# Where the input norm's squares, sums and rotary tables run: ScalarE and VectorE in place of POOL

## The chip, the cores and the metric

The kernel runs on one core of a Trainium2 chip. The core has a matrix engine (TensorE, PE in the profile), VectorE (DVE), ScalarE (ACT), GpSimd (POOL) and a queue engine that issues transfers (SyncE, SP). The metric is the device time of one launch in microseconds, and lower is better. The time quoted is the median of a few runs.

## The reference

An encoder block normalises its input, multiplies it with one wide matrix, and feeds three mixers (dilated window attention, grouped-query attention, attention into a memory), whose gated outputs are projected, merged and projected once more. What matters here is the beginning:

```python
def rms_norm(x, g):
    y = xf * lax.rsqrt(jnp.mean(xf * xf, axis=-1, keepdims=True) + NORM_EPS)
    return (y * g.astype(jnp.float32)).astype(x.dtype)

h = rms_norm(x, g_pre[layer])
a_qkv, bq, bk, bv, mq, ga, gb, gm, mg = jnp.split(h @ w_in[layer], split_at, axis=-1)
...
qb_ = axial_rope(rms_norm(bq.reshape(b, s, B_HEADS, HEAD_DIM), q_norm[layer]), row_pos, col_pos)
kb_ = axial_rope(rms_norm(bk.reshape(b, s, B_KV_HEADS, HEAD_DIM), k_norm[layer]), row_pos, col_pos)
```

`x` has 1024 rows of 1024 channels, in float32. The block needs the sum of squares of each row, and for the second mixer tables of cosine and sine multiplied with the norm weights of queries and keys.

## The kernel before

The input comes transposed, as eight tiles `xk[0]` to `xk[7]` of 128 channels by 1024 rows. Float32 products are made of two parts: each operand is split into a high part (`hh`, `wh`, made by ACT) and the rest (`hl`, `wl`, made by DVE as source minus high part), and three multiplications are added up (high times high, rest times high, high times rest).

**The x stage** is a loop over the eight tiles. For every other tile, `split_wkv` splits a quarter of the key and value weights (`wbh` on ACT, `wbl` on DVE, line 106). Then `x_tile(k)` makes `hh[k]` on ACT (L271) and `hl[k]` on DVE (L272), both scaled by the norm's weight, in two halves of 512 columns. Then `x_sq(k - 1)` squares the tile before, in place, and adds it to `acc`, so that `acc` ends as the sum over the eight channel groups. The first square is written to `acc` itself (L276). Squares of tiles 2 and 4 run on POOL (L279), the others on ACT (L281). The sums of tiles 1, 3, 5, 6 and 7 run on DVE, those of 2 and 4 on POOL (both L282). Behind the loop come the key tables `Ck` and `Sk` on POOL (L464) and the last square and sum, of tile 7. The row scale isn't applied to `x`; it is applied later to what comes out of the multiplications.

**PE meanwhile** runs `kv_proj`: for each tile k, 24 multiplications of 128x256 (eight row blocks times three terms, L373) into four banks. Ahead of those of k = 7 stands `rstd_cols`: eight transposes of `acc` (L258), two reductions on DVE (L259) into `rcol`, and then on POOL scale and offset (L128), the power -1/2 (L130), `rsq` (L380, L381) and `nrcol` (L382).

**Behind it** PE goes on with two gate units. Each is two halves of 24 multiplications of 128x512 into one of two banks `d`. A half is evacuated by DVE (L220, multiplied with `rb`, the row scale as a row), ACT (L221, tanh) and DVE (L222); the third half needs the bank of the first, the fourth that of the second. Woven in between are the norm of the keys, `k_norm` (a square on ACT, L335, a reduction on DVE, L337, four small operations on `kss` on POOL, L338 to L341, and the products with the key tables on DVE, L342 to L346), the transposes that make `rb` (L264, copied by ACT, L423) and the preparation of the memory `mt` (`mh`, `ml`, L393 and L394, its squares on ACT, L395, and sums on POOL, L396 to L399). `kn_mult` then multiplies keys with `kss` (L405) and splits the values (`VS`, L410 and L411). Then eight small units (L537) follow that work on the memory.

**What sets the order.** PE's order is that of the program throughout. For ACT, DVE and POOL the order is the program's from the x stage to the end of the two gate units (`manual_schedule`); what is written behind that, `kn_mult` and the query tables `Cq` and `Sq` (L464) among it, is placed by a scheduler that works with estimated times and may put an operation into a gap ahead of its place in the program. Each engine then works through its instructions in the order fixed beforehand. Loads and stores are issued by SP in order.

Of the kernel before, what the change touches and what calls it, by code (L numbers as in the profile page):

```python
# [10 lines left out]
AF = mybir.ActivationFunctionType  # L11
OP = mybir.AluOpType
# [11 lines left out]
B_COS, B_SIN, B_QN, B_QS, B_KN, B_KS = 0, 512, 170, 234, 298, 362  # L24
# [26 lines left out]
def block(ctx: ExitStack, tc: tile.TileContext, x, xT, memT, cst, msk, bcst, tabA, gpost,  # L51
          wu, wb, wmem, wbr, wout, out):
    nc = tc.nc
    V, A, G, PE = nc.vector, nc.scalar, nc.gpsimd, nc.tensor
# [24 lines left out]
    def pss1():  # L79
        return bank["p"].tile([P, 512], F32, name="s1", tag="s1", bufs=bank["n"][1])  # L80
# [4 lines left out]
    def pso():  # L85
        return bank["p"].tile([P, 512], F32, name="ov", tag="o", bufs=bank["n"][3])
# [11 lines left out]
    rcol = const.tile([P, NT], F32, name="rcol")  # L98
    nrcol = const.tile([P, NT], F32, name="nrcol")
# [27 lines left out]
    def rstd_of(dst, ssq, n, post=None):  # L127
        G.tensor_scalar(dst, ssq, 1.0 / n, EPS, op0=OP.mult, op1=OP.add)  # L128
        w = dst.shape[-1]
        G.tensor_tensor(dst, dst, mhalf[:, :w], op=OP.pow)  # L130
        if post is not None:
            G.tensor_scalar(dst, dst, post, None, op0=OP.mult)
# [70 lines left out]
    fp = {}  # L203
# [48 lines left out]
    xk = [st.tile([P, S], F32, name=f"xk{k}") for k in range(8)]  # L252
    acc = st.tile([P, S], F32, name="acc")

    def cols_of(col, acc, n):
        p = pst()
        for T in range(n):
            PE.transpose(p[:, T, :], acc[:, T * 128:T * 128 + 128], ident)  # L258
        V.tensor_reduce(col, p[:, :n], axis=AX.X, op=OP.add)  # L259
# [14 lines left out]
    def x_sq(k):  # L274
        if k == 0:
            A.activation(acc, xk[k], AF.Square)  # L276
        else:
            if k in P_SQ:
                G.tensor_tensor(xk[k], xk[k], xk[k], op=OP.mult)  # L279
            else:  # L280
                A.activation(xk[k], xk[k], AF.Square)  # L281
            (V if k in V_ADD else G).tensor_tensor(acc, acc, xk[k], op=OP.add)  # L282


    def fetch_wb(c0):
# [77 lines left out]
    def kv_proj():  # L363
        banks = [pss1(), pss1(), pss1(), pso()]
        th, tl = wkv
        for k in range(8):
            if k == 7:
                rstd_cols()
            for T in range(NT):
                dst = banks[T // 2][:, T % 2 * 256:T % 2 * 256 + 256]  # L370
                t = slice(T * 128, T * 128 + 128)
                for i, (a, b) in enumerate([(hh[k][:, t], th[:, k]), (hl[k][:, t], th[:, k]), (hh[k][:, t], tl[:, k])]):
                    PE.matmul(dst, a, b, start=k == 0 and T % 2 == 0 and i == 0, stop=k == 7 and T % 2 == 1 and i == 2)  # L373
        return banks

    def rstd_cols():
        for i in range(2):
            cols_of(rcol[:, 4 * i:4 * i + 4], acc[:, i * 512:i * 512 + 512], 4)
        rstd_of(rcol, rcol, D)
        G.tensor_tensor(rsq, rcol, rcol, op=OP.mult)  # L380
        G.tensor_scalar(rsq, rsq, 1.0 / HD, None, op0=OP.mult)  # L381
        G.tensor_scalar(nrcol, rcol, -1.0, None, op0=OP.mult)  # L382

    mh, mlo, mm, part, kns = [], [], [], [], []

# [15 lines left out]
    def kn_mult(n):  # L401
        t1, ss = part[n]
        kn = st.tile([P, 2, 2, 64], F32, name="kn", bufs=4)
        kns.append(kn)
        V.tensor_tensor(kn, t1, ss[:, :, :, None].to_broadcast([P, 2, 2, 64]), op=OP.mult)  # L405
        for t in range(2):
            T = 2 * n + t
            vv = banks[n].rearrange("q (t h d) -> q t h d", t=2, h=4)[:, t, 2:4]
            r = rcol[:, T:T + 1]
            A.activation(VS[:, T, :, 0:64], vv, AF.Copy, scale=r)  # L410
            V.scalar_tensor_tensor(VS[:, T, :, 64:128], vv, r, VS[:, T, :, 0:64].bitcast(F32),  # L411
                                   op0=OP.mult, op1=OP.subtract)
# [50 lines left out]
    def table(nm, src, gv, E):  # L463
        E.tensor_tensor(tabs[nm], bt[:, src:src + 512].rearrange("p (t d) -> p t d", t=NT),  # L464
                        cs[:, gv:gv + 64][:, None, :].to_broadcast([P, NT, 64]), op=OP.mult)

    for k in range(8):
        if k % 2 == 0:
            split_wkv(k // 2)
        x_tile(k)  # L470
        if k:
            x_sq(k - 1)
    table("Ck", B_COS, B_KN, G)
    table("Sk", B_SIN, B_KS, G)
    x_sq(7)
    banks = kv_proj()
    fp["p"] = st
    add_gate(2, 0)
# [10 lines left out]
        late.append(lambda n=n: kv_out(n, kns[n]))  # L489
    for n in range(4):  # L490
        kn_mult(n)
    table("Cq", B_COS, B_QN, G)
    table("Sq", B_SIN, B_QS, G)

    def mem_norm_a():
        mm.append(st.tile([P, 2], F32, name="col"))
# [780 lines left out]
MN_A, MN_B = 0, 7  # L1277
KV_K = 5
WR, KV_STEP, RB_WAIT, KN_PAD = 2, 700, 1500, 2800.0
V_ADD, P_SQ = (1, 3, 5, 6, 7), (2, 4)  # L1280
LAG_S, LAG_T, LAG_P, LAG_F = 9, 10, 12, 13
BP = 4
B_LEAD, B_PRIO = 1.0, 120
# [118 lines left out]
```

## Time and profile before

| What | us |
|---|---|
| median of 3 runs | 1536.92 |
| their lowest and highest | 1534.99, 1537.64 |
| the profiled execution | 1537.39 |
| its span, first to last instruction | 1535.6 |
| TensorE busy in the span | 1498.6 |
| VectorE, ScalarE, POOL busy | 972.8, 712.7, 443.9 |
| last sum of squares ends | 38.73 |
| gate units begin on PE | 44.92 |
| memory units begin on PE | 68.45 |

The times in the profile count from the first instruction. A timeline row gives the start, the busy time, the engine, the line, the operation with output and inputs, their shapes, how many, and in brackets the idle time before it with what ended it. Busy times of neighbours can overlap by some hundredths, so the step from start to start is a little shorter than the busy time. The granted clock is the share of TensorE's full speed.

### The profile page before, as it was taken

How to read it: one execution, taken by the hardware profiler on the slowest of the kernel's cores; microseconds unless marked ns; L12 is line 12 of the kernel's file. 1: busy time of each engine (PE TensorE's matmuls, PEld its weight loads, DVE VectorE, ACT ScalarE, POOL GpSimd, SP SyncE). 2: the span in 40 equal slices, each digit the busy share in tenths (PEclk: the TensorE clock that was granted, in tenths of full speed). 3: DMA queues.
4: the chain of work that ended last, by engine and by line, in shares of the span. 5: the costliest groups of instructions: out<-in, count | busy, mean ns of one | idle time of the engine just before them, and what ended most of it. 6: DMA issues, size and time to landing. Idle time of an engine off the chain costs nothing.

```text
span 1535.6 us, 20807 instructions
## 1 busy us (share of the span) xinstructions
PE 1498.6 (98%) x7748; PEld 1238.4 (81%) x7748; DVE 972.8 (63%) x1598; ACT 712.7 (46%) x1457; POOL 443.9 (29%) x363
## 2 busy tenths in 40 slices
PE   6999989999999999999999999999999999999998
PEld 5899977777777778888878888887888788888787
DVE  7765469989988985555566466556625442524843
ACT  5453346676666662554446445444642111212321
POOL 4415512444544552211221222122200100233422
PEclk9999999999999999999999999999999999999999
DMA  5332011111112112101121121112126441523332
GB/s 211 95 126 70 29 42 62 56 42 62 53 41 63 62 56 93 41 29 42 45 68 42 42 80 47 42 31 83 42 76 194 164 132 35 204 70 117 124 110 96
DMA packets 55044, 119.79 MB, mean 78 GB/s; under 512 B 13792, under 2 KB 23712, under 8 KB 54816
## 3 DMA queue, kind: packets, MB, share of 16 engines
q1 hardware_dynamic: 54800, 118.34, 23.4%
q8 instruction: 61, 1.00, 0.3%
q14 instruction: 39, 0.32, 0.1%
q10 hardware_dynamic: 144, 0.13, 0.0%
HBM read 96.06 MB, written 22.38 MB: 77 GB/s over the span
## 4 chain that ended last, share of the span: by engine, by line
PE 75%; DVE 11%; issue 4%; ACT 3%; DMA 3%; POOL 2%; SPq 0%; DVEq 0%; POOLq 0%; ACTq 0%
PE d L147 12%; PE d L143 12%; PE d L145 12%; PE sc L125 7%; PE sc L1248 4%; PE s L125 3%; PE sc L147 3%; PE sc L145 3%; PE sc L143 3%; PE ov L989 2%; DVE bpl L106 2%; PE s L709 1%; DVE bn L691 1%; PE ov L730 1%; PE s L708 1%
## 5 line engine op out<-in xcount | busy, mean ns | idle before, releaser
L143 PE MATMUL d<-hh,wh 128*128 128x512 f32 x992 | 396.1, 399 | 1.4 <-DVE fth L222 1.4
L147 PE MATMUL d<-hh,wl 128*128 128x512 f32 x992 | 397.2, 400 | 0.0
L145 PE MATMUL d<-hl,wh 128*128 128x512 f32 x992 | 393.6, 397 | 0.0
L147 PEld LDWEIGHTS d<-hh,wl 128*128 128x128 f32 x992 | 187.1, 189 | 38.5 <-issue 3.6
L143 PEld LDWEIGHTS d<-hh,wh 128*128 128x128 f32 x992 | 187.2, 189 | 38.3 <-DVE fth L222 2.3
L145 PEld LDWEIGHTS d<-hl,wh 128*128 128x128 f32 x992 | 187.1, 189 | 36.2 <-issue 1.0
L105 ACT ACTIVATE wh<-wr 128x1024 fp32r<-128x1024 f32 (+1 forms) x100 | 95.4, 955 | 246.7 <-PE sc L145 108.3
L720 POOL TENSOR_TENSOR bl<-bl,bp 128x512 f32<-128x512 f32 x96 | 135.5, 1412 | 120.4 <-ACT bp L711 112.1
L838 POOL TENSOR_TENSOR rot<-rot,t2a 128x512 f32<-128x512 f32 x48 | 82.6, 1721 | 297.4 <-DVE t2a L837 297.4
L106 DVE TENSOR_TENSOR bpl<-bp,bph 128x512 fp32r<-128x512 f32 x128 | 130.5, 1020 | 23.8 <-ACT bph L105 23.3
L106 DVE TENSOR_TENSOR wl<-wr,wh 128x1024 fp32r<-128x1024 f32 (+1 forms) x100 | 119.0, 1191 | 21.2 <-ACT wh L105 20.5
L1149 POOL TENSOR_TENSOR acc<-acc,th 128x1024 f32<-128x1024 f32 x16 | 45.4, 2837 | 203.8 <-DVE th L1148 203.8
L711 ACT ACTIVATE bp<-s 128x512 f32<-128x512 f32 x128 | 76.2, 595 | 60.0 <-PE s L709 58.2
L947 ACT ACTIVATE pra<-pra,sts 128x128 f32<-128x128 f32 (+2 forms) x152 | 67.2, 443 | 61.9 <-DVE sts L939 61.2
L147 PE MATMUL sc<-hh,wl 128*128 128x512 f32 x224 | 87.8, 392 | 1.8 <-DVE wl L106 1.8
L691 DVE TENSOR_REDUCE bn<-tr 128x1 f32<-128x512 f32 x128 | 86.7, 681 | 4.4 <-PE tr L690 3.9
L143 PE MATMUL sc<-hh,wh 128*128 128x512 f32 x224 | 87.9, 392 | 0.0
L145 PE MATMUL sc<-hl,wh 128*128 128x512 f32 x224 | 87.9, 392 | 0.0
L939 DVE CUSTOM_DVE_ANT_0 pra<-s,mask 128x128 f32<-128x128 f32 (+2 forms) x152 | 48.4, 348 | 61.8 <-PE s L125 49.1
L105 ACT ACTIVATE bph<-bp 128x512 fp32r<-128x512 f32 x128 | 80.9, 632 | 3.5
L835 DVE TENSOR_TENSOR rot<-d,tab 128x512 f32<-128x512 f32 x48 | 33.1, 690 | 67.5 <-PE d L147 67.2
L125 PE MATMUL sc<-gh,wh 128*128 128x512 f32 x192 | 74.7, 389 | 0.0
(278 smaller groups left out, 3096.9 us busy)
## 6 DMA issues: line engine op xcount, KB each, us to landing
wr<-in_wu SPq DMA_DIRECT2D x76, 512.0 KB
g2d<-fth SPq DMA_DIRECT2D x24, 256.0 KB
wgt<-wgd SPq DMA_DIRECT2D x24, 256.0 KB
ot<-od SPq DMA_DIRECT2D x12, 512.0 KB
gt<-g2d SPq DMA_DIRECT2D x12, 512.0 KB
wr<-in_wbr SPq DMA_DIRECT2D x24, 256.0 KB
thd<-fth SPq DMA_DIRECT2D x20, 256.0 KB
th<-thd SPq DMA_DIRECT2D x10, 512.0 KB
```

Of the source, the lines that this page charges most:

```text
L105: A.activation(dst_h, src, AF.Copy)
L106: V.tensor_tensor(dst_l, src, dst_h.bitcast(F32), op=OP.subtract)
L125: PE.matmul(out_ps, a, b, start=i == 0, stop=i == n - 1)
L143: PE.matmul(dst, wh[:, k, :], hh[k][:, t], start=k == 0, stop=False)
L145: PE.matmul(dst, wh[:, k, :], hl[k][:, t], start=False, stop=False)
L147: PE.matmul(dst, wl[:, k, :], hh[k][:, t], start=False, stop=k == 7)
L691: V.tensor_reduce(st[i]["n"][:, j, c:c + 1], s, axis=AX.X, op=OP.min)
L711: A.activation(pp, s, AF.Exp, scale=-1.0)
L720: G.tensor_tensor(lsum[i % 2], lsum[i % 2], pp, op=OP.add)
L838: G.tensor_tensor(o[:, t], o[:, t], t2, op=OP.add)
L947: A.activation(src, raw, AF.Exp, scale=-1.0, bias=bias, accum_out=sts[:, h, 1, T:T + 1])
L1248: PE.matmul(parts[h], *terms[h][j], start=j == 0, stop=j == 23)
```

## The change

In `x_sq` every square but the first runs on ACT and every sum on DVE; the constants that named the tiles are gone. The key tables move from POOL to DVE and behind the last square. The query tables stay on POOL, but the scheduler may place them only behind the norm's last POOL operation, the one that writes `nrcol` (`issue_after` draws an order on the same engine, without a wait).

```diff
@@ x_sq
-            if k in P_SQ:
-                G.tensor_tensor(xk[k], xk[k], xk[k], op=OP.mult)
-            else:
-                A.activation(xk[k], xk[k], AF.Square)
-            (V if k in V_ADD else G).tensor_tensor(acc, acc, xk[k], op=OP.add)
+            A.activation(xk[k], xk[k], AF.Square)
+            V.tensor_tensor(acc, acc, xk[k], op=OP.add)
@@ rstd_cols
-        G.tensor_scalar(nrcol, rcol, -1.0, None, op0=OP.mult)
+        fp["rstd"] = G.tensor_scalar(nrcol, rcol, -1.0, None, op0=OP.mult)
@@ behind the x loop
-    table("Ck", B_COS, B_KN, G)
-    table("Sk", B_SIN, B_KS, G)
     x_sq(7)
+    table("Ck", B_COS, B_KN, V)
+    table("Sk", B_SIN, B_KS, V)
     banks = kv_proj()
@@ behind the gate units
-    table("Cq", B_COS, B_QN, G)
-    table("Sq", B_SIN, B_QS, G)
+    with tc.issue_after(fp["rstd"].ins):
+        table("Cq", B_COS, B_QN, G)
+        table("Sq", B_SIN, B_QS, G)
@@ constants
-V_ADD, P_SQ = (1, 3, 5, 6, 7), (2, 4)
```

## The prediction

> **What bounds the kernel now.** I read the page's busy shares first, then the chain of waits in order of time, then the timelines of VectorE (DVE) and POOL over the first 75 us, then the busy times by stretches. Over the whole span TensorE sets the time:
>
> ```profile
> PE 1498.6 (98%) x7748; PEld 1238.4 (81%) x7748; DVE 972.8 (63%) x1598; ACT 712.7 (46%) x1457; POOL 443.9 (29%) x363
> ```
>
> Nothing after about 70 us is touched by the change, and there PE hardly waits (PE is busy for 1219.6 us of the 1235.6 us behind 300 us). So the question is only when PE's unbroken run begins. The chain, in order of time, says what stands before it (start, duration, what):
>
> ```profile
> 23.22 5.17 DVE hl L272 x2
> 28.38 1.15 DVE wbl L106
> 29.81 3.08 DVE hl L272 x2
> 32.89 2.04 DVE acc L282
> ...
> 36.26 1.15 DVE acc L282
> 37.50 1.24 DVE acc L282
> 38.78 1.98 PE tr L258 x8
> ```
>
> The chain runs on DVE through the x stage, up to the last sum of squares, which ends at 38.73; the transposes of `acc` start PE 0.05 us later. I call that end A. From 38.78 on, PE's idle gaps are a few tenths (0.34 at 62.2, 0.19 at 71.2), so a microsecond off A is a microsecond off the kernel, if what follows A keeps step. DVE is what the x stage waits for, and the reader should compare equal instructions in its timeline (start, busy, line, shape):
>
> ```profile
> 12.28 1.42 DVE L272 SCALAR_TENSOR_TENSOR hl<-xk,cs,hh 128x512 fp32r<-128x512 f32 x2 [0.39 <-ACT hh L271]
> 13.84 2.91 DVE L282 TENSOR_TENSOR acc<-acc,xk 128x1024 f32<-128x1024 f32 x1
> 16.67 3.56 DVE L272 SCALAR_TENSOR_TENSOR hl<-xk,cs,hh 128x512 fp32r<-128x512 f32 x2
> ...
> 20.76 1.40 DVE L272 SCALAR_TENSOR_TENSOR hl<-xk,cs,hh 128x512 fp32r<-128x512 f32 x2
> 22.08 1.21 DVE L282 TENSOR_TENSOR acc<-acc,xk 128x1024 f32<-128x1024 f32 x1
> ```
>
> The same pair of `hl` takes 1.4 us or 3.1 to 5.2 us, the same sum 1.21 or 2.91. POOL's timeline tells which:
>
> ```profile
> 13.77 1.90 POOL L279 TENSOR_TENSOR xk<-xk 128x1024 f32<-128x1024 f32 x1 [13.35 <-DVE hl L272]
> 16.89 2.79 POOL L282 TENSOR_TENSOR acc<-acc,xk 128x1024 f32<-128x1024 f32 x1 [1.22 <-DVE acc L282]
> 22.24 2.81 POOL L279 TENSOR_TENSOR xk<-xk 128x1024 f32<-128x1024 f32 x1 [2.56 <-DVE hl L272]
> 25.13 2.71 POOL L282 TENSOR_TENSOR acc<-acc,xk 128x1024 f32<-128x1024 f32 x1
> 27.80 1.54 POOL L464 TENSOR_TENSOR Ck<-bt,cs 128x512 f32<-128x512 f32 x1
> ...
> 32.31 1.55 POOL L464 TENSOR_TENSOR Sq<-bt,cs 128x512 f32<-128x512 f32 x1
> ```
>
> Every long DVE row lies under a wide POOL row, and every short one in a POOL gap. It isn't the loads: the short rows at 20.76 and 22.08 ran with DMA at about 400 GB/s, the long ones behind 28 us with DMA at zero. The stretch sums to 11.05 us: sums 2.91 and 2.12 against 1.21 (1.70 and 0.91), `hl` pairs 3.56, 5.17 and 3.08 against 1.42 (2.14, 3.75, 1.66), a `wbl` 1.58 against 0.69 (0.89).
>
> **The change, part by part.** *Squares 2 and 4 to ScalarE.* Two more activations of 1.06 us (L281's row). ACT has the room: it waits 3.47, 4.11, 2.22 and 2.30 us for DVE in this stage. *Sums 2 and 4 to DVE.* Two of 1.21 us, on the path. *The four wide POOL operations and the tables leave the stage*, and with them the 11.05 us of stretch. DVE gains about 11.05 - 2.42 = 8.6 us.
>
> I check this by walking the stage with unstretched steps from start to start (`hl` pair 1.33, sum 1.14, `wbl` 0.61, from the rows at 20.15 to 23.22). The start of sum 1 at 13.84 stays, since its square ends at 13.81. Then: `hl3` 14.98, sum 2 16.31, `wbl` 17.45, `hl4` 18.06, sum 3 19.39, `hl5` 20.53, sum 4 21.86, `wbl` 23.0, `hl6` 23.6, sum 5 24.9, `hl7` 26.1, sum 6 27.4. The last square must wait for `hl7` (27.4) and takes 1.06, so sum 7 runs from 28.6 to 29.8. ACT with 1.25 + 0.97 + half of 0.6 = 2.5 us for each tile stays ahead of DVE's 2.8. PE: 138 of the 168 multiplications of k = 0 to 6 are left at 13.33, at 0.118 us each, so they end at 29.6. PE and DVE arrive together, and A moves from 38.73 to 29.8: **8.9 us**. The loads are in time: everything issued by 10.4 us (5.5 MB with weights and constants) has been moved by about 17.5 us, and the last tile is wanted at 24. The second weight tile for the gates is issued when `wbl` frees its buffer, now at 23.6, and took 3.5 us (29.91 to 33.4) before; ACT wants it at about 29. On SP only the two `mt` loads stand ahead of it (13.54 and 16.8, which wait for squares 0 and 1), and behind it the loads of 42.64, whose buffers come free later.
>
> *Key tables to DVE*, behind the last sum: no row shows this operation on DVE. The nearest is L106's 128x512 with two SBUF inputs, 0.69 us; from below its step of 0.60, from above POOL's own 1.54. I take 0.66 a step, so 1.3 us (1.2 to 3.1). Queued behind them is the first reduction of the transposes (L259), which before began 1.20 us behind A because it waited for PE. So about 0.1 to 0.2 us shows, and that is made up: the second reduction waited for PE too (0.16) and now doesn't. Priced 0; uncovered they cost 1.3, at the upper end 1.9 more than the cover.
>
> *PE's clock.* The stretch 35 to 45 us shows a granted clock of 0.66:
>
> ```profile
> 35.00:45.00 10.00, 6.22 (x33) 6.22 (x34) 8.49 (x13) 3.73 (x5) 3.35 (x2) 0.66 0.14 39
> ```
>
> PE had stood for 4.3 us, and ran the 24 multiplications of k = 7 at 0.21 us each (40.40 to 44.92) instead of 0.118. With a gap of only 0.2 us they take 2.84, the eight transposes about 0.95 instead of 1.62. PE would reach the gate units at 29.85 + 0.95 + 2.84 = 33.6 instead of 44.92: a lead of 11.3 us, 2.4 more than A's. I give it no credit, because the fourth half unit doesn't wait for PE: at 62.57 it waits for DVE's `fth` L222, the end of a chain from A (reduction, POOL's rstd, `kss`, DVE's `kn`, the first evacuation, then DVE without a pause). PE's 2.4 us become idle time there.
>
> *Query tables behind the norm.* This is the one real cost. Until now they lay at 30.8 to 33.9; now they can't start before `nrcol` L382, which before ended at 46.19. POOL works its queue in order, and next in it is `kss` L338 (46.16), whose input had been there since 44.07. Where the tables land isn't in the trace. At best they fall into POOL's later gap of 3.87 us (50.06 to 53.93) and cost nothing. At worst both stand directly behind `nrcol` and each `kss` is 2 x 1.53 = 3.05 us late. I take the second. The order is drawn up beforehand by the scheduler from its own estimates, and these take POOL's small operations for shorter than they are: it put the first `kn` ahead of L346 (48.13, 48.47), where DVE in fact waited 1.81 us for `kss`. By such estimates POOL has nothing to do behind `nrcol` while DVE still works on two `wl` (2.35 us) ahead of the `kss` reductions, and it put both tables into the first such gap before. Then the second `kss` ends at 50.06 - 8.9 + 3.05 = 44.2, and `kn` L405 behind it on DVE, with the evacuation L220 queued behind that. Before, a 0.35, a wait of 0.18 and another 0.35 us of `VS` lay between `kn` and L220 (50.53 to 51.48); these don't need `kss` and can be done while DVE waits. So L220 starts at about 44.2 + 0.35 = 44.5, where 51.48 - 8.9 = 42.6 would keep step: **1.9 us late**, and the 11.0 us from there to the end of the second L222 follow unchanged. POOL's mem norm hangs on the same DVE rows and moves with them.
>
> [...]
>
> The sum: 8.9 - 1.9 = 7.0 us. The profiled execution took 1537.39 (span 1535.6 and 1.8 around it), 0.47 above the median of the runs, 1536.92. So 1530.4 for the former, **1529.9** for the median.
>
> **The rivals.** *The tables find a gap.* POOL's 3.87 us speak for it; the order of the queue decides. Gain 8.9, time 1528.0. *PE's lead is kept.* If the DVE order behind A closes up its own waits (1.81 at 46.3, 0.94 at 49.2), L222 comes 2.4 us earlier and the warm clock counts: 11.3, time 1525.6. Against it: the wait for `kss` is POOL's, and it grows. *No change.* The x stage gets shorter but the evacuation chain doesn't, say because `kss`, `kn` and rows stretched under the tables give back over 6 us: this needs both full tables and four DVE rows stretched by a whole table, 3.05 + 4 x 1.53 = 9; about 1537. *Slower: the stretch isn't POOL's.* If DVE's long rows come from something that stays, DVE only gets work: two sums of 1.21, 0.1 of the key tables beyond their cover, and the 1.9 behind A: 4.4 us, time 1541.3. It decides once more than 11.05 - 2.42 - 1.9 = 6.7 us of stretch stay, that is with the six `hl` pairs of k = 2 to 7 above 1.42 + 1.1 = 2.5 us. Against it stands the match row by row with POOL.
>
> **How the numbers follow.** Forecast (gain 4.5 to 8) 60%; tables in a gap 20%; lead kept 6%; no change 5%; slower 9%. A change under 0.2% (3.1 us) can't be told from none in this kernel, whose three runs span 2.6 us. So faster 0.86, same 0.05, slower 0.09. The range goes from 1525.5 (the lead kept) to 1534.0 (both tables at 3.05 uncovered and two rows stretched by 1.5, gain 2.9); what is left out is slower, no change and the tails, 2 in 10.
>
> **What would show it.** Right: `hl` pairs at 1.3 to 1.45 throughout, `acc` ending near 29.8, no stretch of low clock at 35 to 45, `kss` L338 about 3 us behind `nrcol`, a PE gap of 1 to 3 us in front of the third or fourth half unit, and the first `kv` units (L537) about 7 us earlier. Wrong: `hl` rows still of 2 us, or a new wait between A and the evacuations larger than 4 us, or waits for other engines appearing behind 75 us.

## The result, and the profile after

The changed kernel takes 1529.93 us (median of 4 runs, 1528.06 to 1530.81) where the kernel before took 1536.64 (median of 4, the three runs above and one more; 1534.99 to 1537.64). The ratio is 0.9962, with a 95% interval of 0.995 to 0.9974. The forecast was 1529.9, a gain of 7.0 us; 6.7 was measured. The profiled execution has a span of 1527.2 us instead of 1535.6.

In the x stage, VectorE's timeline of the changed kernel (start, busy, line, shape; L279 is the sum that was L282):

```profile
21.21 1.41 DVE L272 SCALAR_TENSOR_TENSOR hl<-xk,cs,hh 128x512 fp32r<-128x512 f32 x2
22.54 1.22 DVE L279 TENSOR_TENSOR acc<-acc,xk 128x1024 f32<-128x1024 f32 x1
...
28.06 2.55 DVE L279 TENSOR_TENSOR acc<-acc,xk 128x1024 f32<-128x1024 f32 x2
30.52 0.68 DVE L461 TENSOR_TENSOR Ck<-bt,cs 128x512 f32<-128x512 f32 x1
```

Every pair of `hl` now takes 1.41 or 1.42 us, every sum 1.22 or 1.23, and the last sum ends at 30.61 instead of 38.73. Behind the norm, POOL's timeline:

```profile
37.48 0.23 POOL L379 TENSOR_SCALAR nrcol<-rcol 128x8 f32<-128x8 f32 x1
37.69 1.09 POOL L461 TENSOR_TENSOR Cq<-bt,cs 128x512 f32<-128x512 f32 x1
38.74 1.09 POOL L461 TENSOR_TENSOR Sq<-bt,cs 128x512 f32<-128x512 f32 x1
39.79 0.20 POOL L335 TENSOR_TENSOR kss<-kss,rsq 128x4 f32<-128x4 f32 x1
```

Both query tables lie directly behind `nrcol`, and `kss` waits for them. VectorE waits for `kss` in turn (rows of `kn` and of the first evacuation; L402 was L405):

```profile
41.76 0.42 DVE L402 TENSOR_TENSOR kn<-kt,kss 128x256 f32<-128x256 f32 x1 [3.91 <-POOL kss L338]
...
45.11 0.68 DVE L220 TENSOR_TENSOR fth<-d,rb 128x512 f32<-128x512 f32 x1
```

What this does further on is in TensorE's timeline (only rows with a wait, given in brackets):

```profile
47.20 0.50 PE L143 MATMUL d<-hh,wh 128*128 128x512 f32 x1 [0.74 <-DVE fth L222]
56.14 0.74 PE L143 MATMUL d<-hh,wh 128*128 128x512 f32 x1 [3.21 <-DVE fth L222]
```

These are the first multiplications of the third and the fourth half unit. Before, only the fourth waited, and only 0.18 us (its step from the row ahead was 0.34 us longer than usual):

```profile
62.57 0.50 PE L143 MATMUL d<-hh,wh 128*128 128x512 f32 x1 [0.18 <-DVE fth L222]
```

The changed kernel's row at 56.14 lasts 0.74 us instead of 0.50, for a reason that the busy times by stretch show. Each line has the stretch, its length, the busy time and number of instructions of TensorE, its weight loads, VectorE, ScalarE and POOL, and then granted clock, DMA share and GB/s:

```profile
50.00:55.00 5.00, 2.94 (x13) 2.08 (x12) 5.00 (x11) 4.07 (x8) 3.25 (x5) 1.00 0.01 2
55.00:60.00 5.00, 3.86 (x10) 3.05 (x11) 4.47 (x10) 2.22 (x5) 2.24 (x2) 0.66 0.57 157
60.00:65.00 5.00, 5.00 (x31) 4.34 (x30) 1.48 (x3) 1.55 (x2) 1.97 (x4) 1.00 0.14 52
```

The stretch of low clock that lay at 37 us before is gone, but a new one of 3.4 us follows the new wait (56.2 to 59.6 us, at a granted clock of 0.50).

PE's order is the same in both kernels, so the n-th multiplication of one can be set against the n-th of the other. How much earlier the changed kernel's starts are, in us:

| Place on PE | before at | earlier by |
|---|---|---|
| transposes of `acc` (L258) | 38.78 | 8.1 |
| gate units | 44.9 | 10.5 |
| third half unit | 56.8 | 9.6 |
| fourth half unit | 62.57 | 6.4 |
| transposes for `mbc` (L264) | 71.40 | 4.8 |
| 214 us | 214.3 | 4.6 |
| 232 us | 232.0 | 6.3 |
| 1189 us | 1189.2 | 5.6 |
| 1204 us | 1204.2 | 7.8 |
| the last | 1529.1 | 8.3 |

From 71 to 214 us next to nothing is won or lost (0.2 us). The jumps of 1.7 at 215 to 230 and 2.2 at 1190 to 1204 come from the clock for the most part: the kernel before had it halved for 6.8 and 3.4 us there in its profiled execution, the changed one for 3.4 us and not at all. Between 232 and 1000 us 0.9 us is lost again, 0.7 of it in one wait for VectorE at 325 us. So of the 8.3 us between the two profiled executions about 4.8 come from the start; the medians, the changed kernel's over runs with mean granted clocks of 0.994 to 0.997, differ by 6.7.

### The profile page after: what moved, and what is told of

Same layout as the page of the kernel before. It is cut to its first block, busy times and chain, and to the rows that moved or that the text cites. A ratio compares the mean times of both kernels' runs of the same rounds, so it can differ in the third digit from the quotient of the medians.

```text
span 1527.2 us, 20804 instructions
## 1 busy us (share of the span) xinstructions
PE 1493.5 (98%) x7748; PEld 1233.9 (81%) x7748; DVE 966.0 (63%) x1602; ACT 713.5 (47%) x1459; POOL 429.8 (28%) x357
## 4 chain that ended last, share of the span: by engine, by line
PE 77%; DVE 10%; issue 4%; ACT 4%; POOL 3%; DMA 3%; SPq 0%; DVEq 0%; POOLq 0%; ACTq 0%
PE d L147 12%; PE d L143 12%; PE d L145 12%; PE sc L125 7%; PE sc L1246 4%; PE s L125 3%; PE sc L147 3%; PE sc L143 3%; PE sc L145 3%; PE ov L987 2%; DVE bpl L106 2%; PE ov L728 2%; PE s L707 1%; PE s L706 1%; PE ov L727 1%
## 5 line engine op out<-in xcount | busy, mean ns | idle before, releaser
L106 DVE TENSOR_TENSOR wl<-wr,wh 128x1024 fp32r<-128x1024 f32 (+1 forms) x100 | 119.0, 1190 | 21.5 <-ACT wh L105 20.8
```

The source lines that it names most:

```text
L106: V.tensor_tensor(dst_l, src, dst_h.bitcast(F32), op=OP.subtract)
```

## Experiments: which part does it

Two kernels split the change. In the first, squares and sums are moved and all four tables stay on POOL without a tie; in the second, only the tables are moved.

```diff
 x3_squares_only, against the changed kernel
+    table("Ck", B_COS, B_KN, G)
+    table("Sk", B_SIN, B_KS, G)
     x_sq(7)
-    table("Ck", B_COS, B_KN, V)
-    table("Sk", B_SIN, B_KS, V)
...
-    with tc.issue_after(fp["rstd"].ins):
-        table("Cq", B_COS, B_QN, G)
-        table("Sq", B_SIN, B_QS, G)
+    table("Cq", B_COS, B_QN, G)
+    table("Sq", B_SIN, B_QS, G)
```

```diff
 x4_tables_only, against the kernel before
-    table("Ck", B_COS, B_KN, G)
-    table("Sk", B_SIN, B_KS, G)
     x_sq(7)
+    table("Ck", B_COS, B_KN, V)
+    table("Sk", B_SIN, B_KS, V)
...
-    table("Cq", B_COS, B_QN, G)
-    table("Sq", B_SIN, B_QS, G)
+    with tc.issue_after(fp["rstd"].ins):
+        table("Cq", B_COS, B_QN, G)
+        table("Sq", B_SIN, B_QS, G)
```

> Only the squares and sums are moved; all four tables stay on POOL, free. Theory: VectorE loses the stretch under POOL's squares and sums but keeps up to 3.5 us under the tables, and kss isn't delayed: 1.4 us slower than the changed kernel, 1530.5 to 1532.5, with the last sum ending at 33 to 34.5. Rival (any POOL work in the stage costs as much as before): the last sum at 36 or later, 1534 or more.

> Only the tables are moved (keys to VectorE behind the last sum, queries tied behind the norm); squares and sums of tiles 2 and 4 stay on POOL. Theory: 3.5 us of stretch go, 2.1 come back at kss: about 1.4 us faster than before, 1534.5 to 1536, the last sum at 35 to 36. Rival (the gain is the tables'): 1532 or less.

Squares alone: 1530.3 us, ratio to before 0.9959 (0.9946 to 0.9971). Tables alone: 1534.68, ratio 0.9992 (0.9983 to 1.0002). The last sums end at 33.5 and 35.5, as the theory had them; the time of squares alone lies 0.2 us below its range. That the tables alone gain anything isn't shown, since their interval takes in 1. Without the tie, the tables start as soon as their input has landed. POOL's timeline with squares alone, then VectorE's of the same time:

```profile
20.16 1.48 POOL L461 TENSOR_TENSOR Ck<-bt,cs 128x512 f32<-128x512 f32 x1 [19.74 <-DMA bt<-in_bcst]
21.60 1.55 POOL L461 TENSOR_TENSOR Sk<-bt,cs 128x512 f32<-128x512 f32 x1
```

```profile
20.59 3.10 DVE L272 SCALAR_TENSOR_TENSOR hl<-xk,cs,hh 128x512 fp32r<-128x512 f32 x2
23.62 2.12 DVE L279 TENSOR_TENSOR acc<-acc,xk 128x1024 f32<-128x1024 f32 x1
```

The pair of 1.41 us takes 3.10, the sum of 1.22 takes 2.12. So nearly the whole gain is the squares' and sums'. The tables' move alone won 3.3 us at the transposes of `acc`, had 1.6 left at the fourth half unit, behind the late `kss`, and 0 behind the stretch of low clock that followed the wait there (61.4 to 64.8 us).

The third kernel keeps the key tables on VectorE and only takes away the tie:

```diff
-    with tc.issue_after(fp["rstd"].ins):
-        table("Cq", B_COS, B_QN, G)
-        table("Sq", B_SIN, B_QS, G)
+    table("Cq", B_COS, B_QN, G)
+    table("Sq", B_SIN, B_QS, G)
```

> The changed kernel without the tie: the two query tables are free and stand first in POOL's queue, so they run in the x stage, as soon as their input has landed. Theory (POOL stretches VectorE's two-input rows, and the tie costs 2.1 us at the first kss): the x stage gets 1 to 2 us longer (before, four tables stretched 3.5 us), kss comes 2.1 us earlier relative to the last sum, so the time stays within 1 us of the changed kernel (1529.0 to 1531). Rival (what helped is the tie, or tables in the x stage cost their whole 3 us): 1532 or more.

1529.37 us (0.9959, 0.9946 to 0.9972): no difference from the changed kernel that the spread of the runs would show. The two tables stretch one pair to 2.25 and one sum to 2.12 us, 1.7 us together, the last sum ends at 31.95, and `kss` follows `nrcol` at once. The tie exchanges one cost for another of about the same size. The places differ in the clock too: in this kernel's profile it was halved from 32.0 to 35.4 us and not behind the fourth half unit's wait.

## Experiments: why VectorE is stretched

To measure the stretch by itself, four POOL instructions of 128x512 were added to the changed kernel's x stage, each on a tile whose sum has just been taken. No result uses them. In one kernel they fill, in the other they multiply.

```diff
 x7_memset
             x_sq(k - 1)
+        if 3 <= k < 7:
+            G.memset(xk[k - 1][:, 0:512], 0.0)
 x8_mult
             x_sq(k - 1)
+        if 3 <= k < 7:
+            h = xk[k - 1][:, 0:512]
+            G.tensor_tensor(h, h, h, op=OP.mult)
```

> The changed kernel with four POOL fills of 128x512 added in the x stage, each on a tile whose sum has just been taken (they read nothing; no result uses them). Theory (POOL stretches VectorE only while it reads SBUF): the hl pairs stay at 1.4 us, the last sum ends at 30 to 31, as without them. Rival (any POOL instruction that writes SBUF stretches): each pair under a fill is 0.4 us or more longer.

> The same at the same places with POOL multiplications of 128x512 (two reads) in place of the fills. Theory: the pair of hl that starts with each takes 0.8 to 1.0 us longer, the last sum ends 3 to 4 us later than in the changed kernel, 33.5 to 35. Rival (the stretch belongs to wide 1024 instructions or to several in a row): under 0.3 us each.

POOL's and VectorE's rows under a fill, then the same under a multiplication:

```profile
20.11 0.53 POOL L471 MEMSET xk<- 128x512 f32 x1 [2.54 <-DVE acc L279]
```

```profile
19.96 1.41 DVE L272 SCALAR_TENSOR_TENSOR hl<-xk,cs,hh 128x512 fp32r<-128x512 f32 x2
```

```profile
21.87 1.48 POOL L472 TENSOR_TENSOR xk<-xk 128x512 f32<-128x512 f32 x1 [2.42 <-DVE acc L279]
```

```profile
21.72 2.19 DVE L272 SCALAR_TENSOR_TENSOR hl<-xk,cs,hh 128x512 fp32r<-128x512 f32 x2
```

Two of the fills lay under a pair, which stays at 1.41, and two under a `wbl`, which stays at 0.69. Under a multiplication each of the four pairs takes 2.19 or 2.20, 0.78 us more, and the x stage 3.1 us more (the last sum ends at 33.46 against 29.37, of which 0.96 was there ahead of the first multiplication, by later loads). The kernels took 1530.12 and 1533.12 us in single runs. As far as these rows go the theory holds: a POOL fill, which only writes and lasts 0.53 us, left VectorE's times as they were, a multiplication, which reads as well and lasts 1.42 to 1.48 us, added 0.78 us, and one instruction at a time was enough. Whether the reads or the length make the difference, the two kernels don't separate. (The stretch is at the lower edge of the 0.8 to 1.0 us expected. Each fill began while a VectorE instruction was running and ended before it, and the next one began at most 0.07 us before the fill's end; one that begins early in a fill isn't tried.) POOL pays for the overlap too: the tables took 1.54 us each before, beside VectorE's two-input work, and take 1.09 behind `nrcol`, where VectorE waits.

The single instructions of the traces show how the two hold each other up. In the x stages of the kernel before, x1, x3, x4 and x8, a two-input VectorE instruction began 22 times while a two-input POOL instruction was running. It always ended 0.55 us (128x512) or 1.08 us (128x1024) after POOL's, however early it had begun. One that began first kept its own time, 0.74 or 1.21 us, and POOL's instruction took longer instead, as the tables above. So what VectorE paid in these rows is what was left of POOL's instruction at that moment, less 0.2 us: 0.98 us left cost an `hl` 0.78 us more in x8, 2.35 us left cost one 2.15 us more in the kernel before.

## Experiments: what the 2.1 us behind the norm are worth

The query tables are wanted only behind 100 us (in the kernel before, from 109.4 us on). Two kernels put them further back: behind POOL's last sum of the memory's squares, and behind the last operation of the memory's norm, the power of `col`. A third adds that the first split of a memory weight on VectorE (`wl`, L509), which the scheduler had put ahead of the evacuation that the fourth half unit waits for, goes behind it. A fourth has only this last edit. `fp["macc"]`, `fp["col"]` and `fp["ev"]` hold the operations behind which these edits put others, the last one the L222 of the second half unit. The changed kernel was measured again, without an edit (a2), beside the split alone (x9) and both together (x10, the kernel of x6). The split and that evacuation in the changed kernel:

```profile
53.34 2.15 DVE L509 TENSOR_TENSOR wl<-wr,wh 128x1024 fp32r<-128x1024 f32 x1
55.41 0.68 DVE L222 SCALAR_TENSOR_TENSOR fth<-d,fth 128x512 f32<-128x512 f32 x1
```

```diff
 x2_tables_macc
-    with tc.issue_after(fp["rstd"].ins):
+    with tc.issue_after(fp["macc"].ins):
 x5_tables_after_col, in mem_norm_b
         V.tensor_copy(mm[3], rows_of(mm[2], 2))
+        with tc.issue_after(fp["col"].ins):
+            table("Cq", B_COS, B_QN, G)
+            table("Sq", B_SIN, B_QS, G)
 x9_wl_only, in kv_prep (x6, x10: with x5's edit)
-        V.tensor_tensor(wl, raw, wh.bitcast(F32), op=OP.subtract)
+        with tc.issue_after(fp["ev"].ins):
+            V.tensor_tensor(wl, raw, wh.bitcast(F32), op=OP.subtract)
```

> The changed kernel with the query tables tied behind POOL's last sum of the memory's squares instead of behind the norm. Theory (the fourth half unit waits for a chain through kss, and the 2.1 us of the two tables in it are lost): kss follows nrcol at once, the wait in front of the fourth half unit falls from 3.2 to 1.0 to 1.6 us, the drop of the granted clock behind it is gone, and the time is 1.7 to 3.5 us below the changed kernel: 1526.5 to 1528.2. Rival (the tables only move the wait: col L128 now queues behind them and PE waits for mbc): no change, 1529.5 to 1530.5, with PE waiting about 2 us at L264.

> The changed kernel with the query tables tied behind the last POOL operation of the memory's norm (the power of col), so that they fall into POOL's idle time behind 65 us. Theory: kss follows nrcol at once, as in the kernel with the tables behind the memory's sums (there the fourth half unit waited 2.1 us, and PE then 1.1 at L264 for col); the second wait is gone. PE's place at the eight memory units is 4 us ahead of the changed kernel, 9 ahead of before. If a shift there passes whole to the end, the time is 1526 to 1528. Rival (a part of it is taken up later, by stretches of lower clock around 215 us that come whatever the start is): the place at 71 us is 4 ahead, and the time still 1528.5 to 1530.

> The one before, with the first memory weight split on VectorE (wl, about 2.2 us, stretched by POOL's sums) put behind the evacuation L222 of the second half unit instead of ahead of it. Theory (VectorE's chain to that L222 sets when the fourth half unit starts): L222 starts 1.5 to 2.1 us earlier against the last sum, PE's wait there falls from 2.1 to under 0.7 us, and the time is 1.5 to 2 us below the one before: 1524.5 to 1526.5. Rival (ACT's tanh or the mem norm becomes the wait): PE waits the same 1.5 to 2 us at another place, no change in the time.

> The changed kernel again, on one chip with the next two. 1528.5 to 1531; the wait in front of the fourth half unit 3.2 us; whether a stretch of lower clock follows it depends on where that wait falls in the clock's fixed windows of 3.4 us.

> The changed kernel with only the first memory weight split put behind the evacuation L222; the query tables stay tied behind the norm. Theory: the wait in front of the fourth half unit falls from 3.2 to about 1.5 us, no stretch of lower clock follows it, and PE reaches the memory units 1.7 us earlier than the changed kernel where that has no such stretch: 1.5 to 3 us below it in the median, 1526.5 to 1528.5. Rival (the wait only moves to POOL's sums of the memory): less than 0.7 us.

> Both moves again (split behind the evacuation, query tables behind the memory's norm), beside the changed kernel on one chip. Theory: 2 to 4 us below the changed kernel, 1525.5 to 1528. Rival (the earlier median of 1527.45 was the chip's): within 1 us of the changed kernel.

| Kernel | time, us | ratio to before (95%) | wait of 4th half unit | L264 earlier than before by |
|---|---|---|---|---|
| changed, first batch | 1529.93 | 0.9962 (0.995, 0.9974) | 3.21 | 4.8 |
| a2: changed, again | 1530.70 | 0.9971 (0.9961, 0.998) | 3.18 | 5.7 |
| x2: behind the sums | 1529.14 | 0.9953 (0.9941, 0.9965) | 2.12 | 8.0 |
| x5: behind the norm | 1530.59 | 0.9969 (0.9956, 0.9981) | 2.28 | 7.8 |
| x9: split only | 1529.16 | 0.9955 (0.9942, 0.9967) | 1.39 | 7.5 |
| x6: both | 1527.45 | 0.9949 (0.9935, 0.9964) | 0.32 | 9.8 |
| x10: both, again | 1529.13 | 0.9954 (0.9941, 0.9967) | none | 9.2 |

The waits show the mechanism. TensorE's rows with a wait, of x2, of x9 and of x6:

```profile
53.62 0.50 PE L143 MATMUL d<-hh,wh 128*128 128x512 f32 x1 [2.12 <-DVE fth L222]
63.35 0.43 PE L264 MATMUL tr<-cs,col 128*128 128x128 f32 x2 [1.11 <-POOL col L130]
```

```profile
53.90 0.50 PE L143 MATMUL d<-hh,wh 128*128 128x512 f32 x1 [1.39 <-DVE fth L222]
61.00 0.44 PE L260 MATMUL tr<-cs,macc 128*128 128x128 f32 x2 [1.36 <-POOL macc L398]
```

```profile
51.53 0.50 PE L143 MATMUL d<-hh,wh 128*128 128x512 f32 x1 [0.32 <-DVE fth L222]
58.66 0.44 PE L260 MATMUL tr<-cs,macc 128*128 128x128 f32 x2 [1.37 <-POOL macc L398]
```

With the tables out of the way, the fourth half unit waits a microsecond less than in the changed kernel, and with the split behind the evacuation as well it hardly waits at all. Each time a part of what is won is taken at the next place: in x2 by `col`, queued behind the tables (1.11 us), in x6 and x9 by POOL's sums of the memory (1.4 us). PE's place at L264 moves from 4.8 us ahead of before to as much as 9.8.

The times follow only in part. x2 and x5 missed what was expected of them: PE was 2 to 3 us further ahead at L264 than in the changed kernel, and the medians are 0.8 lower and 0.7 higher than its first. x6 was to take 1524.5 to 1526.5 and took 1527.45; its repetition x10 was 1.6 us below the changed kernel on the same chip, just short of the 2 to 4 expected; x9 was 1.5 us below it, the least expected, and at 1529.16 outside its range of times. The rival of x5, that something later takes it up, is borne out in the profiled executions for one term: around 215 us the changed kernel had one stretch of low clock of 3.4 us in both of its profiles, while x2, x5, x6 and x10 had one of 6.8, which is 1.7 us of PE's time. That is not enough for x5, whose runs lie between 1526.61 and 1534.66; what makes them spread so far stays open. The kernel with both edits had the lowest median of its batch both times (x9 only 0.03 us behind it), 2.5 us below the changed kernel's first and 1.6 below its second, but the intervals of the ratios overlap with the changed kernel's, so that it is faster still is likely and not shown.

## Why the prediction was right

- **The bound and the stretch: right.** Loads came later in the changed kernel's profile (the second tile's `hh` starts at 9.53 instead of 8.36), so A ended at 30.6 instead of the 29.8 of the walk: 8.1 us won, not 8.9. In its other profile, a2, it was 8.9. Two readings behind it were loose. Not every short row lay in a POOL gap: the sum at 22.08 took its 1.21 us beside POOL's square of 22.24, having begun first, and the square took 2.81 instead of the 1.90 of the one at 13.77. And the loads were not all away from the long rows: from 29.81 to 32.90 us the DMA share was 0.49, and beside the short sum at 22.08 only 121 GB/s moved. The long pair at 23.22, with a share of 0.07 from 22.2 to 28 us, and x8 carry the argument.
- **Key tables at nothing: right.** 0.68 us each; the reduction behind them starts at 31.73, and the two reductions end 2.4 us behind A instead of 2.75.
- **Query tables: right in place, too dear in size.** They lie directly behind `nrcol`, by the argument about the scheduler's estimates. They took 1.05 us a step and not 1.53, since the price came from rows that were themselves stretched: `kss` is 2.1 us late, not 3.05.
- **How late the evacuation gets: right in size, by another sum.** L220 starts at 45.11, which is 6.4 us earlier than before, so 1.75 us late against A; 1.9 was forecast from 3.05 less 1.2 us of `VS` done in the wait. The scheduler put `VS` where it was, and nothing of the 2.1 was made up but 0.35, by the earlier reductions. That the tables stretch rows on VectorE there by 1.5 us each, as the upper end of the range has it for two rows, no run shows: in the changed kernel VectorE stood still from 37.8 to 41.8, waiting for `kss`, while the tables ran from 37.69 to 39.83.
- **PE's lead becomes idle time: right.** PE was 10.5 us ahead at the gate units and 6.4 at the fourth half unit, after waits of 0.74 and 3.21, the second a little over the 1 to 3 us named as a sign.
- **What was left out of the sum.** The wait of 3.2 us, forecast as harmless idle time, was followed by a granted clock of 0.50 from 56.2 to 59.6 us, and the multiplications there came every 0.43 us instead of every 0.23: another 1.6 us, from 6.4 to 4.8. So the memory units (L537, now L535) began 5.0 us earlier, at 63.45, and not the 7 named as a sign. The prediction had read this price in the row at 35 to 45 us and used it only to say that the stretch would go. That the median nevertheless came to the forecast to 0.1 us is partly luck: on another chip the changed kernel gained 4.4 against the runs of before there (a2), on the first 6.7. In the profiled execution the start gave 4.8 of 8.3 us, and part of the rest came from stretches of low clock that fell differently near 220 and 1195 us, which the sum doesn't have.
- **The rivals.** The slower one, that the stretch isn't POOL's, fell with the first `hl` row. No change fell with the time, whose interval ends at 0.9974. The tables in a gap didn't happen by themselves; x2 and x5 made it happen and won a microsecond of wait. PE's full lead came about only with another edit, in x6 (11.0 us at the fourth half unit).

## What to carry to other kernels

Before work is put on POOL because POOL is idle, look at what VectorE does at that time: in the kernel before, its two-input work beside POOL's squares, sums and tables lost 11.05 us against its short rows (1.42 us a pair, 1.21 a sum), where the two sums cost 2.4 us on VectorE itself. With the squares and sums alone moved (x3) the last sum ended 5.2 us earlier than before, although VectorE had taken over those 2.4 us. Price a moved operation from a row in which its neighbours are quiet, as they will be at its new place. And a wait on TensorE can cost more than its own length: here one of 3.21 us was followed by 3.4 us at a granted clock of 0.50, 1.6 us more, and one of 2.12 us, in x2, by none. Look for that in the granted clock behind the wait.

## What the runs showed of the clock

The trace records when the granted clock changes. In the kernel before it changed at 37.15, 43.97, 221.47, 228.29, 1194.27 and 1197.68 us, at distances that are whole multiples of 3.413 us, and in all 13 profiled executions the changes in the start phase lie on such a grid of 3.41 us. It lies differently in executions of one kernel: the low stretch behind the fourth half unit's wait begins at 56.2 us in the changed kernel's first profile, 0.1 us behind the start of the multiplication that ends the wait, and at 55.2 in a2, 0.2 us ahead of it. The windows of that grid, up to 75 us, in which PE stood still for over 55%, and the three next to them; PE's rows are taken with their modelled ends:

```
kernel   window, us     PE idle   clock halved at its end
before   33.7 to 37.1   79%       yes
after    52.8 to 56.2   94%       yes
a2       51.8 to 55.2   88%       yes
x1       28.6 to 32.0   77%       yes
x4       58.0 to 61.4   90%       yes
x5       50.7 to 54.1   67%       yes
x7       52.0 to 55.4   83%       yes
x8       55.4 to 58.8   76%       yes
x8       31.5 to 35.0   58%       yes
x10      27.1 to 30.5   58%       yes
x2       49.8 to 53.2   50%       no
x3       52.9 to 56.4   46%       no
x3       29.0 to 32.5   44%       no
```

No other window up to 75 us in which the clock was full had more than 42%. So up to there a full window with 58% or more was followed by a halved one in these executions, and one with 50% or less by a full one. Behind 75 us one with 52.5% was followed by a halved one too, in the kernel before from 1190.9 to 1194.3. Behind a halved window the clock was still halved in the kernel before, where PE had stood for 14.7% of it (221.5 to 224.9), and full in the changed kernel, where it had stood for 9.1% (216.7 to 220.1): the stretches near 215 us lasted 6.8 and 3.4 us there. x10 had the clock halved after a wait of 1.97 us (its stretch from 30 to 35 us):

```profile
30.00:35.00 5.00, 4.63 (x26) 4.64 (x27) 4.85 (x7) 1.60 (x3) 1.88 (x2) 0.66 0.00 0
```

and x2 kept it after 2.12 us that fell across two windows. A wait of 1.97 us was thus followed by a window at half clock, which is 1.7 us of PE's time, and one of 2.12 us by none. That goes some way to explain why runs of one kernel differ by 3 us and more: of a2's the one of 1534.36 us had a mean granted clock of 0.993, the one of 1528.86 us 0.996.
